# Seven block products instead of eight for the output projections of the long set in a hybrid mLSTM and attention layer

## The chip, the cores and the metric

One core of one Trainium2 chip runs the whole layer. The metric is the device time of one execution, in microseconds (us): 2188.01 us before the change, the median of 3 runs (2187.36 to 2189.47).

## What is computed

The layer is applied to two sets of tokens with the same weights: A, the long set (1024 tokens), and B, the short set (512 tokens). Cut to what matters here:

```python
h = rms_norm(x, pre_w)
cols = einsum('bsd,dc->bsc', h, w_in)                 # d = 1024, some 11,000 columns
y_m = mlstm_mixer(...) * silu(m_z)                    # 1024 wide, two directions
y_a = dilated_attention(...) * silu(a_z)              # 512 wide, three groups of heads
p_m = einsum('bsc,cd->bsd', y_m, w_pm)                # 1024 x 1024
p_a = einsum('bsc,cd->bsd', y_a, w_pa)                #  512 x 1024
g = sigmoid(gate)
merged = g[:, :, 0] * p_m + g[:, :, 1] * p_a
out = einsum('bsd,de->bse', merged, w_out)            # 1024 x 1024
return x + rms_norm(out, post_w)
```

All is float32. The kernel writes each factor of a product as hi + lo, two numbers of TensorE's input type, and computes hi·hi + hi·lo + lo·hi: three matmuls for one (`mm3`, L230). Such a pair is made by ScalarE (ACT: hi is a rounded copy) and VectorE (DVE: lo = x − hi).

## The kernel before, in words

**First stage.** It multiplies A's normed tokens by `w_in`. Here the seven block products of a 2x2 block product (Strassen's scheme in Winograd's form) are already used: a "pair" of column units is one block row of weights, A's two blocks of 512 tokens are the other side, and `unit_pair` (L788) forms seven products of 4 k-tiles each, adding and subtracting their outputs with DVE. The sums of weight blocks that the scheme needs are made on GpSimd (POOL) in `pair_weights` (L768, sums at L782 to L785) and `unit_pair` (L800), from two raw loads `pw_raw`. Eight of these pairs, called "zo", hold A's gates z and o.

**Later stages.** The mLSTM of A, attention of A (`attend`), mLSTM of B (`quad`), attention of B, and `combine`, which mixes B's three attention groups (small operations L2033 to L2043 and mixes L2050, L2056 on DVE, turns on TensorE at L2061). They have many short dependent operations, so TensorE (PE) is kept busy with dense products in between. `Fill` (L137) hands these out in *steps*: one step is one k-tile of a dense product, three matmuls of 128x512. `STEPS` says how many steps go beside each stage, `SHORT` is where the short set's part of `w_in` ends.

The last 512 steps hold the output projections, in this order: A's first 512 tokens, A's second, B. For each block of 512 tokens:
- `proj_m` (in `branches`, L2174): 64 steps, 8 output tiles of 8 k-tiles. The weight unit is 128 x 1024 (512 KB), loaded by POOL's queue into one of two `wraw` buffers and split into a hi and a lo tile (L296 on ACT, L302 on DVE) from a ring of pairs. Each output is evicted by DVE with its gate (L2200).
- `proj_a`: 32 steps, 8 outputs of 4 k-tiles; three DVE operations and an ACT copy for each (L2217 to L2220) make the merged tile's hi and lo.
- `final` (L2239): 64 steps, 8 outputs; for each tile of 128 tokens the two halves are squared on ACT (L2261), multiplied by the norm's weights on DVE as they are evicted (L2263, L2268), the root is taken on POOL (L2267), and two DVE operations add the residual `xo` (L2271).
- `split` (L2129) loads the rows of y and splits them to hi and lo (L2144 on ACT, L2145 on DVE). `along` (L2155) runs such a generator beside the steps of another product: the rows of the next block beside `final`, one every 3 steps.

Dense outputs rotate over two PSUM tiles during attention and over four during B's `combine`. PE's and SP's instructions are issued in the order in which the code is written; those of DVE, ACT and POOL are placed by a scheduler before the run. On each engine the resulting order is fixed: an instruction that waits holds up all behind it.

Of the kernel before, what the change touches and what calls it, by code (L numbers as in the profile page):

```python
# [29 lines left out]
P = 128  # L30
# [174 lines left out]
class Net:  # L205
    def __init__(self, tc, a):
        self.tc, self.nc, self.a = tc, tc.nc, a
        self.clock = self.lag = 0
        self.deep, self.zeros = 1, []
        self.pending, self.owner = [], {}  # L210
        self.defer, self.mixed, self.rows = False, set(), {}
        self.queued, self.pace = [], 1
        self.side = self.nc.sync
        self.lows = None
        self.scans, self.state, self.keyed, self.held, self.sum = [], [], [], [], None
        self.low_part = None
        self.retired = []
        self.narrow, self.acc, self.direct = {}, [None, None], {}
# [568 lines left out]

    def unit_pair(self, weights, H, sb, cp, ps):  # L788
# [189 lines left out]
    def short_units(self, T):  # L978
# [30 lines left out]
        def gate(br, ct):  # L1009
            def use(p):  # L1010
                t = w()
# [1113 lines left out]
    def place(self, which, i, dt=F32R):  # L2125

        return self.take((("V0b", "V1b", "K0", "K1"), ("H0", "H1", "H2", "H3"))[which][i], dt).rearrange("p (k t) -> p k t", k=4)
# [27 lines left out]
    def along(self, units, make, every):  # L2155
# [3 lines left out]
        def wrap(u, last):  # L2159
            def go(weights):  # L2160
                if "g" not in got:
                    got["g"], got["n"] = make(), 0
# [9 lines left out]
        return [wrap(u, u is units[-1]) for u in units]  # L2172

    def branches(self, T, b, odd, before):  # L2174
# [48 lines left out]
        return (self.along(before, lambda: self.split(T, b, 0, [(odd, 0, 1), (odd, 2, 1)], yb, 2 if len(before) > 1 else 3), 3)  # L2223
# [15 lines left out]
    def final(self, T, b):  # L2239
# [4 lines left out]
        def make(weights):  # L2244
            sb = self.osb
            fill = weights.__self__
            self.flush(lambda p: p[3] is not None and p[3][0] is self.sw)
            o = [x[F32] for x in self.sw.bufs]
# [59 lines left out]
STEPS = (316, 260, 192, 290, 86)  # L2308


def body(tc, a):
# [3 lines left out]
    with ExitStack() as st:  # L2315
# [5 lines left out]
        B = Tokens(dram, 512, a[x2], a[y2], "b")  # L2321
        N.constants(N.const)
# [5 lines left out]
        with ExitStack() as s1:  # L2328
# [83 lines left out]
            with ExitStack() as s4:  # L2412
# [16 lines left out]
                with ExitStack() as s3:  # L2429
# [3 lines left out]
                    for kind, i in ([("att", j) for j in range(0, 24, 2)]  # L2433
# [6 lines left out]
                        c = N.unit_pair(weights, H, sb, cp, ps)  # L2440
                        v = [x[:, 1:1 + A.S] for x in c]
# [29 lines left out]
        with ExitStack() as s1:  # L2471
# [35 lines left out]
            with ExitStack() as s2:  # L2507
                sp = N.pool(s1, "sp", 1, "right")
                N.sw = Rot(N, [sp.tile([P, BLK], F32R, name=f"sw{i}") for i in range(4)])
# [29 lines left out]
            extra = [N.take(x) for x in ("X0", "Q1")]  # L2539
            N.wsplit[:0] = [[x[:, 1024 * i:1024 * (i + 1)] for i in range(2)] for x in extra]  # L2540
# [4 lines left out]
            N.postw = None  # L2545
# [21 lines left out]
            N.flush(lambda p: True)  # L2567


def _layout(i):  # L2570
# [13 lines left out]
    def gate_bias(n):  # L2584
# [10 lines left out]
        "w_pm": units(f("w_proj_m")[0], KT), "w_pa": units(f("w_proj_a")[0], 4).reshape(4, 2, P, 4 * P).transpose(0, 2, 1, 3).reshape(4, P, KT * P), "w_out": f("w_out")[0].reshape(4, 2, P, 2, 512).transpose(3, 0, 2, 1, 4).reshape(8, P, KT * P),  # L2595
        "conv": np.concatenate([f("m_conv_w")[0], f("m_conv_b")], 0).reshape(4, 16, P).transpose(2, 1, 0),
# [23 lines left out]
```

## Time and profile before

| | |
|---|---|
| Time, median of 3 (range) | 2188.01 us (2187.36 to 2189.47) |
| Span of the profiled execution | 2185.1 us; the page gives no time of its own for this execution |
| Median less span | 2.9 us |
| TensorE busy | 2173.5 us (99%), 11626 matmuls |
| VectorE / ScalarE / GpSimd busy | 1460.8 (67%) / 1085.1 (50%) / 704.2 us (32%) |
| Weight loads for the outputs | 512 KB each, 24 of `w_pm` and 24 of `w_out` |

The rows name engine, line, operation and tile. "Busy" is time with an instruction in flight; matmuls overlap each other (a 128x512 matmul shows a duration of 389 to 406 ns, while the next starts sooner), so their rate is read from start to start. The same holds, less so, for DVE.

### The profile page before, as it was taken

How to read it: one execution, taken by the hardware profiler on the slowest of the kernel's cores; microseconds unless marked ns; L12 is line 12 of the kernel's file. 1: busy time of each engine (PE TensorE's matmuls, PEld its weight loads, DVE VectorE, ACT ScalarE, POOL GpSimd, SP SyncE). 2: the span in 40 equal slices, each digit the busy share in tenths (PEclk: the TensorE clock that was granted, in tenths of full speed). 3: DMA queues.
4: the chain of work that ended last, by engine and by line, in shares of the span. 5: the costliest groups of instructions: out<-in, count | busy, mean ns of one | idle time of the engine just before them, and what ended most of it. 6: DMA issues, size and time to landing. Idle time of an engine off the chain costs nothing.

```text
span 2185.1 us, 33611 instructions
## 1 busy us (share of the span) xinstructions
PE 2173.5 (99%) x11626; PEld 1857.3 (85%) x11626; DVE 1460.8 (67%) x2927; ACT 1085.1 (50%) x2228; POOL 704.2 (32%) x989
## 2 busy tenths in 40 slices
PE   9999999999999999999999999999999999999998
PEld 8988888888888888888888889999788888888887
DVE  8766564657778555547888775574668855656674
ACT  7322333444444343446777656666756544554332
POOL 1000332333333222326776650011045522232331
PEclk9999999999999999999999999999999999999999
DMA  3642454733333222367646558877668786776772
GB/s 139 193 139 73 146 162 144 227 110 116 107 115 114 75 82 97 135 216 261 202 164 225 175 167 262 240 241 196 203 233 278 248 288 205 229 261 187 242 240 106
DMA packets 205748, 395.62 MB, mean 181 GB/s; under 512 B 36393, under 2 KB 117993, under 8 KB 205578
## 3 DMA queue, kind: packets, MB, share of 16 engines
q1 hardware_dynamic: 175272, 281.39, 40.2%
q0 software_dynamic: 26704, 99.50, 13.8%
q10 hardware_dynamic: 3602, 12.59, 1.4%
q8 instruction: 92, 1.51, 0.3%
q14 instruction: 78, 0.64, 0.1%
HBM read 274.71 MB, written 118.69 MB: 180 GB/s over the span
## 4 chain that ended last, share of the span: by engine, by line
PE 97%; DVE 1%; ACT 1%; DMA 1%; issue 0%; POOL 0%; DVEq 0%; POOLq 0%; ACTq 0%
PE d L233 14%; PE d L235 14%; PE d L234 14%; PE dense L233 13%; PE dense L234 13%; PE dense L235 13%; PE lg L1801 2%; PE pt L1831 2%; PE o L1874 1%; PE num L233 1%; PE num L235 1%; PE num L234 1%; PE num L1494 1%; PE o L1853 1%; PE a L1201 1%; PE kv L233 1%
## 5 line engine op out<-in xcount | busy, mean ns | idle before, releaser
L233 PE MATMUL dense<-H,wh 128*128 128x512 f32 x664 | 269.3, 406 | 0.0
L234 PE MATMUL dense<-H,wh 128*128 128x512 f32 x664 | 260.3, 392 | 0.0
L235 PE MATMUL dense<-H,wl 128*128 128x512 f32 x664 | 260.2, 392 | 0.0
L233 PE MATMUL d<-Hh,phla 128*128 128x512 f32 x608 | 236.5, 389 | 0.0
L235 PE MATMUL d<-Hh,phla 128*128 128x512 f32 x608 | 236.5, 389 | 0.0
L234 PE MATMUL d<-Hl,phla 128*128 128x512 f32 x608 | 236.5, 389 | 0.0
L302 DVE TENSOR_TENSOR wl<-wraw,wh 128x1024 fp32r<-128x1024 f32 (+1 forms) x121 | 150.8, 1248 | 57.9 <-ACT wh L296 57.8
L235 PE MATMUL d<-Hh,phlb 128*128 128x512 f32 x456 | 177.4, 389 | 0.0
L233 PE MATMUL d<-Hh,phlb 128*128 128x512 f32 x456 | 177.4, 389 | 0.0
L234 PE MATMUL d<-Hl,phlb 128*128 128x512 f32 x456 | 177.4, 389 | 0.0
L296 ACT ACTIVATE wh<-wraw 128x1024 fp32r<-128x1024 f32 (+1 forms) x124 | 128.1, 1036 | 62.1 <-PE dense L234 24.3
L235 PEld LDWEIGHTS dense<-H,wl 128*128 128x128 f32 x664 | 124.7, 188 | 28.1
L782 POOL TENSOR_TENSOR psum_w<-pw_raw 128x512 f32<-128x512 f32 x38 | 56.7, 1492 | 271.1 <-DMA pw_raw<-w_in 259.9
L1820 DVE CUSTOM_DVE_ANT_0 ls<-lg,bias 128x256 f32<-128x256 f32 (+2 forms) x240 | 78.7, 350 | 90.3 <-PE lg L1801 61.7
L233 PEld LDWEIGHTS dense<-H,wh 128*128 128x128 f32 x664 | 125.0, 188 | 16.4 <-issue 1.2
L234 PEld LDWEIGHTS dense<-H,wh 128*128 128x128 f32 x664 | 125.2, 189 | 14.7
L235 PEld LDWEIGHTS d<-Hh,phla 128*128 128x128 f32 x608 | 114.1, 188 | 23.7
L234 PEld LDWEIGHTS d<-Hl,phla 128*128 128x128 f32 x608 | 114.1, 188 | 23.7
L233 PEld LDWEIGHTS d<-Hh,phla 128*128 128x128 f32 x608 | 114.1, 188 | 23.7
L800 POOL TENSOR_TENSOR psum_w<-pw_raw,psum_w 128x512 f32<-128x512 f32 x38 | 49.3, 1298 | 254.2 <-DVE phla L764 254.2
L1824 ACT ACTIVATE ls<-ls,nm 128x256 f32<-128x256 f32 (+1 forms) x192 | 87.3, 456 | 70.2 <-DVE nm L1822 47.0
L233 PE MATMUL d<-v,Hh 128*128 128x484 f32 (+1 forms) x336 | 121.3, 361 | 0.1
(665 smaller groups left out, 5838.8 us busy)
## 6 DMA issues: line engine op xcount, KB each, us to landing
pw_raw<-w_in SPq DMA_DIRECT2D x76, 512.0 KB, 3.9
wraw<-w_in SPq DMA_DIRECT2D x63, 512.0 KB, 4.4
aqk_a<-pwk SPq DMA_DIRECT2D x32, 512.0 KB, 6.7
wraw<-w_pm POOLq DMA_DIRECT2D x24, 512.0 KB, 5.9
wraw<-w_out POOLq DMA_DIRECT2D x24, 512.0 KB, 3.7
Q<-aqk_a SPq DMA_DIRECT2D x20, 512.0 KB, 6.3
wraw<-w_v POOLq DMA_DIRECT2D x22, 430.0 KB, 6.5
aqk_b<-sw SPq DMA_DIRECT2D x36, 256.0 KB, 7.2
```

The lines of the kernel that those rows point to most:

```text
L233: nc.tensor.matmul(out, lh, rh, start=start, stop=False, **kw)
L234: nc.tensor.matmul(out, lh, rl, start=False, stop=False, **kw)
L235: nc.tensor.matmul(out, ll, rh, start=False, stop=stop, **kw)
L296: high = nc.scalar.activation(hi[:, :n], raw[:, :n], AF.Copy)
L302: low = (self.lows or nc.vector).tensor_sub(lo[:, :n], raw[:, :n], hi[:, :n].bitcast(F32))
L782: self.nc.gpsimd.tensor_add(s[:, 0], ws[1][:, 0], ws[1][:, 1])
L800: nc.gpsimd.tensor_sub(s[:, 1], wa[:, 1], s[:, 1])
L1201: nc.tensor.matmul(p[:, c - c0], kT[:, ct, c * P:(c + 1) * P], qT[:, ct, c * P:(c + 1) * P], start=ct == 0, stop=ct == 1)
L1801: nc.tensor.matmul(lg[:, hh], q[hh][:, qs], z.rearrange("p (n j) -> p n j", j=P)[:, pair], start=z is k[hh], stop=z is not k[hh])
L1820: nc.vector.tensor_tensor_reduce(out=ls[rows, hh], in0=ts["lg"][hh][rows, of], in1=bt[rows, hh, by], scale=1.0, scalar=NEG, op0=OP.add, op ...
L1824: self.held = self.held[-3:] + [nc.scalar.activation(ls[:, hh], ls[:, hh], AF.Exp, bias=nm[:, hh:hh + 1], accum_out=ot[:, 128 + hh:129 + hh])]
L1831: nc.tensor.transpose(pp[:, hh * nk + x], ts["ls"][:, hh, x * P:(x + 1) * P], self.ident)
```

## The change

`proj_m` and `final` of A are no longer done for each block of 512 tokens. A new function `outputs` does both token blocks at once as a 2x2 block product: for `proj_m`, seven products of 4 outputs and 4 k-tiles (112 steps where there were 128); then `proj_a` for both blocks, with one split of each of its four weight units (64 steps, as before); then `final`, again 112 steps where there were 128. In all there are 1248 steps instead of 1280, and the entry of `STEPS` for B's attention goes from 290 to 258.

- The four sums of weight quadrants for each of the two matrices are made in the first stage by `output_sums`, called in each of the eight "zo" pairs: two loads of 512 KB into `pw_raw` buffers, four POOL operations of 128x512, three stores to a DRAM tile `q_sums`. The raw quadrants come as a new input `w_q`, a rearranged copy of `w_pm` and `w_out`.
- The activations' sums are made on POOL (`combined`, L2248 of the new file, 16 operations of 128x512 for each projection), and every combination is then split by `divide` (ACT L2233, DVE L2234): 28 pieces for each projection, in a ring of 6 places.
- Each product's output is evicted to partial sums: on DVE at L2435 to L2444 in `final`, where one tile can need two additions. Squares, norm and residual follow in `square` (L2414, L2415) and `close` (L2420 to L2424).
- The tiles `mg` (two) hold both the junk output of the squares and one half of the finished tile.
- `place` names other buffers; the four `sw` tiles become one tile and serve as one more pair of the weight ring, where there were two more (X0, Q1).
- B's rows are split beside the new `final`, one every 2 steps from step 86 of its 112.

The diff, cut:

```diff
+    def output_sums(self, i, sb, wk):
...
+        s = wk().rearrange("p (a c) -> p a c", a=2)
+        nc.gpsimd.tensor_add(s[:, 0], wb[:, 0], wb[:, 1])
+        nc.gpsimd.tensor_sub(s[:, 1], s[:, 0], wa[:, 0])
+        nc.gpsimd.tensor_sub(wb[:, 0], wa[:, 0], wb[:, 0])
+        nc.gpsimd.tensor_sub(wa[:, 1], wa[:, 1], s[:, 1])
+        nc.sync.dma_start(self.qs_sums[0:2, u, :, c].rearrange("q p c -> p q c"), s)
...
-    def along(self, units, make, every):
+    def along(self, units, make, every, skip=0):
...
+                    got["g"], got["n"] = make(), -skip
                 for _ in u.make(weights):
-                    if got["n"] % every == 0:
+                    if got["n"] >= 0 and got["n"] % every == 0:
                         next(got["g"], None)
...
+    def outputs(self, T, before):
...
+        def divide(into, key, at, x):
+            hi, lo = at
+            nc.scalar.activation(hi, x, AF.Copy)
+            nc.vector.tensor_sub(lo, x, hi.bitcast(F32))
+            into[key] = at
...
+            jobs += parts(0, a0)
+            two = parts(1, b0)
+            jobs += two[:2] + sums(sub, a1, b1, a1) + two[2:] + sums(add, a0, a0, a1) + parts(2, a0) + sums(sub, b0, b0, a0)
+            jobs += parts(3, a1) + sums(sub, a1, b1, a0)
+            jobs += parts(4, b0) + parts(5, a1) + parts(6, b1)
...
+        def final(weights):
...
+            def square(b, h, t, y, engine):
+                junk = sb.tile([P, S], F32, name="mg", bufs=2)
+                nc.scalar.activation(junk, y, AF.Square, accum_out=ss[b][:, t, h:h + 1])
+                engine.tensor_mul(y, y, pw[:, h * S:(h + 1) * S])
...
+            def evict(i, t, ps):
+                q, r = u[:, t], x[:, t]
+                if i == 0:
+                    nc.scalar.activation(q, ps, AF.Copy)
+                elif i == 1:
+                    self.evicted = add(o[:, t], q, ps)
+                    square(0, 0, t, o[:, t], nc.gpsimd)
+                elif i == 3:
+                    self.evicted = add(r, q, ps)
+                elif i == 4:
+                    y = sb.tile([P, S], F32, name="mg", bufs=2)
+                    self.evicted = add(y, r, ps)
+                    square(0, 1, t, y, nc.vector)
+                    close(0, t, (o[:, t], y))
+                else:
+                    if i == 5:
+                        add(r, r, ps)
+                    self.evicted = add(q, q, ps)
+                    if i == 5:
+                        square(1, 1, t, r, nc.gpsimd)
+                    if i == 6:
+                        square(1, 0, t, q, nc.vector)
+                        close(1, t, (q, r))
...
-        return (self.along(before, lambda: self.split(T, b, 0, [(odd, 0, 1), (odd, 2, 1)], yb, 2 if len(before) > 1 else 3), 3)
+        return (self.along(before, lambda: self.split(T, b, 0, [(odd, 0, 1), (odd, 2, 1)], yb, 3), 2, 86)
...
-STEPS = (316, 260, 192, 290, 86)
+STEPS = (316, 260, 192, 258, 86)
...
+                        if kind == "zo":
+                            N.output_sums(i, sb, w)
...
-            finals = [N.final(*x) for x in ((A, 0), (A, 1), (B, 0))]
-            units = short[:-4] + N.branches(A, 0, 0, short[-4:])
-            units += N.branches(A, 1, 1, finals[:1]) + N.branches(B, 0, 0, finals[1:2]) + finals[2:]
+            last = N.final(B, 0)
+            first, final = N.outputs(A, short[-4:])
+            units = short[:-4] + first + N.branches(B, 0, 0, [final]) + [last]
```

Where the instructions stand. First DVE near the end of A's `final`, beside `combine` of B, in the kernel before. `dense` are the PSUM outputs, `mg` and `sw` the two halves of a finished tile, `xo` the residual, `Q0` and `az1` belong to `combine`:

```order
L2266 SCALAR_TENSOR_TENSOR ss_19916<-ss_19916 128x1
L2268 TENSOR_TENSOR mg_20270<-dense_20197,postw_18670 128x512
L2056 TENSOR_TENSOR Q0_20056<-Q0_20056 128x512
L2271 SCALAR_TENSOR_TENSOR xo00_17492<-sw1_7265,ss_19916,xo00_17492 128x512
L2271 SCALAR_TENSOR_TENSOR xo01_17493<-mg_20215,ss_19916,xo01_17493 128x512
L302 TENSOR_TENSOR wl2_7153<-wraw1_7147,wh2_7152 128x1024
L2063 TENSOR_TENSOR az1_20052<-tp2_20301,az1_20052 128x512
L2056 TENSOR_TENSOR Q0_20056<-Q0_20056 128x512
```

There is one eviction for each output, and a row of B is not split here: that was done beside earlier steps. The same place in the changed kernel, where `dense_20070` is the first and `dense_20177` the last of the fifth product's four outputs, `dense_20302` the last of the sixth's, `dense_20338` the first of the seventh's, and `K0<-ymr0,X0` (L2168) is the lo half of a row of B:

```order
L302 TENSOR_TENSOR wl2_7250<-wraw0_7243,wh2_7249 128x1024
L2168 TENSOR_TENSOR K0_20259<-ymr0_17585,X0_20258 128x512
L2057 TENSOR_TENSOR wd8_20240<-cw8_20235,V0a_20110 128x24
L2444 TENSOR_TENSOR H1_19560<-H1_19560,dense_20338 128x512
L2415 TENSOR_TENSOR mg_20167<-mg_20167,postw_19565 128x512
L2420 SCALAR_TENSOR_TENSOR ss_19563<-ss_19563 128x1
L2438 TENSOR_TENSOR mg_20199<-H0_19562,dense_20177 128x512
L2058 TENSOR_TENSOR wd8_20240<-wd8_20240 128x8
L302 TENSOR_TENSOR wl0_7246<-wraw1_7244,wh0_7245 128x1024
L2443 TENSOR_TENSOR H0_19562<-H0_19562,dense_20302 128x512
L2444 TENSOR_TENSOR H1_19560<-H1_19560,dense_20302 128x512
```

Outputs are now evicted out of turn (`dense_20177` after `dense_20338`), the norms of the fifth product's tiles have moved in among the sixth's and seventh's evictions, and B's rows stand between them. A little later, still on DVE in the changed kernel, stand the last lo halves of B's rows, `H2<-…,H3` (L2168), three ahead of and one behind the norms and mixes:

```order
L302 TENSOR_TENSOR wl1_7248<-wraw1_7244,wh1_7247 128x1024
L2168 TENSOR_TENSOR H2_20261<-sraw_7362,H3_20260 128x512
L2168 TENSOR_TENSOR H2_20261<-ymr0_17585,H3_20260 128x512
L2168 TENSOR_TENSOR H2_20261<-ymr1_17586,H3_20260 128x512
L2424 SCALAR_TENSOR_TENSOR gab_19568<-H1_19560,ss_19564,gab_19568 128x512
...
L2069 TENSOR_TENSOR X1_20112<-V0a_20110,cw8_20496 128x512 x3
L302 TENSOR_TENSOR H0_20477<-wraw1_7244,H0_20477 128x1024
L2168 TENSOR_TENSOR H2_20261<-sraw_7362,H3_20260 128x512
```

These four moved from a place well ahead of A's last evictions to one behind them. On PE, the product that reads them is B's first of `proj_m`, `dense_20487`, right behind A's last output `dense_20434`:

```order
L235 MATMUL dense_20434<-wh1_7247,V1b_19358 128x512
L233 MATMUL dense_20487<-X0_20258,wh2_7249 128x512
L234 MATMUL dense_20487<-K0_20259,wh2_7249 128x512
...
L234 MATMUL dense_20487<-H2_20261,wh2_7249 128x512
L235 MATMUL dense_20487<-H3_20260,wl2_7250 128x512
```

In PE's order 153 matmuls of 128x512 and one turn of four 128x128 lie between the last matmul of `dense_20070`, the fifth product's first output, and the last k-tile of `dense_20487`.

More of the change, by code (lines that the diff above doesn't have):

```diff
@@ L2246, in make @@
             fill = weights.__self__
-            self.flush(lambda p: p[3] is not None and p[3][0] is self.sw)
-            o = [x[F32] for x in self.sw.bufs]
+            o = self.four("V0b")
+            o = [o[:, i] for i in range(4)]
             ss = sb.tile([P, 4, 8], F32, name="ss", bufs=2)
@@ L2321, in body @@
         B = Tokens(dram, 512, a[x2], a[y2], "b")
+        N.qs_sums = dram.tile([4, 4, P, 1024], F32, name="q_sums")
         N.constants(N.const)
@@ L2544, in body @@
             N.xo_bufs = [(i, [N.osb.tile([P, BLK], F32, name=f"xo{i}{j}") for j in range(2)]) for i in range(2)]
-            N.postw = None
+            N.late, N.postw = Rot(N, [x for _, two in N.xo_bufs for x in two]), None
             N.attend(B, fill, STEPS[3], kept["qkv"], ("lg", "o", "pt"), 7)
```

261 lines of the change are left out of this document (254 added, 7 removed).

## The prediction

> **What bounds the kernel now.** I read the page first, then TensorE's waits, then the windows, then single rows.
>
> ```profile
> span 2185.1 us, 33611 instructions
> PE 2173.5 (99%) x11626; PEld 1857.3 (85%) x11626; DVE 1460.8 (67%) x2927; ACT 1085.1 (50%) x2228; POOL 704.2 (32%) x989
> PE   9999999999999999999999999999999999999998
> PE 97%; DVE 1%; ACT 1%; DMA 1%; issue 0%; POOL 0%; DVEq 0%; POOLq 0%; ACTq 0%
> ```
>
> PE is busy in every slice and is 97% of the chain. Its waits say the same:
>
> ```profile
> engine line waited for: us in total, times, longest us
> PE d L2370 <- DMA Hh<-prew: 2.3, 1, 2.3
> PE d L476 <- ACT Hh L470: 0.5, 1, 0.5
> PE d L420 <- DVE u2b L417: 0.5, 1, 0.5
> PE d L235 <- DVE Hl L472: 0.4, 1, 0.4
> ```
>
> All are at the start. So a matmul that goes is time that goes, as long as the others keep up. How close they come is in the windows (after the length: busy us of PE, PEld, DVE, ACT, POOL, then the granted clock):
>
> ```profile
> 450.00:600.00 150.00, 150.00 (x663) 124.20 (x663) 111.61 (x115) 63.63 (x65) 51.53 (x51) 1.00 0.30 106
> 750.00:800.00 50.00, 50.00 (x222) 41.42 (x221) 28.59 (x34) 18.42 (x20) 14.40 (x12) 1.00 0.21 74
> 1050.00:1200.00 150.00, 149.95 (x911) 132.83 (x910) 125.47 (x249) 108.13 (x257) 106.13 (x169) 1.00 0.61 202
> 1850.00:1900.00 50.00, 50.00 (x278) 43.39 (x278) 34.99 (x90) 26.99 (x72) 14.51 (x27) 1.00 0.72 236
> 2060.00:2080.00 20.00, 20.00 (x93) 16.54 (x92) 17.91 (x34) 5.84 (x9) 9.09 (x17) 1.00 0.85 266
> 2160.00:2186.00 26.00, 17.82 (x79) 14.44 (x77) 8.70 (x16) 2.75 (x8) 3.34 (x6) 0.91 0.31 118
> ```
>
> In B's `combine`, from 2060 on, DVE is busy 17.9 of 20 us: the next bound stands there, hidden so far.
>
> **What goes.** 1280 steps become 1248: 32 steps of three matmuls, 96 in all. The first window has 663 matmuls in 150 us, 0.226 us each; near the outputs the starts lie as far apart:
>
> ```profile
> 1900.88 0.39 PE L235 MATMUL dense<-Q,K 128*128 128x512 f32 x1
> 1901.11 0.39 PE L233 MATMUL dense<-Q,K 128*128 128x512 f32 x1
> 1901.33 0.39 PE L234 MATMUL dense<-Q,K 128*128 128x512 f32 x1
> ```
>
> 96 x 0.227 = 21.8 us, all from the path. An output of `final` had 8 steps (24 matmuls, 5.4 us) and has 4 (12 x 0.227 = 2.7 us). The eight weight splits that go (40 for A become 32) lie beside PE and give nothing by themselves.
>
> **What comes, first stage.** Four POOL additions and three stores in each of eight pairs, where POOL has 14.4 of 50 us busy. One addition:
>
> ```profile
> L800 POOL TENSOR_TENSOR psum_w<-pw_raw,psum_w 128x512 f32<-128x512 f32 x38 | 49.3, 1298 | 254.2 <-DVE phla L764 254.2
> ```
>
> A pair is 7 x 4 x 3 = 84 matmuls, 19 us; POOL gets 4 x 1.3 = 5.2 us more in it, about 11 instead of 5.5. The raw loads of the next pair queue behind on the shared buffers, one pair later than now; POOL and SP still have half a pair free. I take 0, and 2 us as the upper end.
>
> **What comes, outputs: DVE's queue.** DVE's prices, start to start, are in B's `combine`:
>
> ```profile
> 2064.58 0.15 DVE L2266 SCALAR_TENSOR_TENSOR ss<-ss 128x1 f32<-128x1 f32 x1
> 2064.65 0.69 DVE L2268 TENSOR_TENSOR mg<-dense,postw 128x512 f32<-128x512 f32 x1
> 2065.25 0.69 DVE L2056 TENSOR_TENSOR Q<-Q 128x512 f32<-128x512 f32 x1
> 2065.85 0.75 DVE L2271 SCALAR_TENSOR_TENSOR xo<-sw,ss,xo 128x512 f32<-128x512 f32 x1
> 2066.51 0.75 DVE L2271 SCALAR_TENSOR_TENSOR xo<-mg,ss,xo 128x512 f32<-128x512 f32 x1
> 2067.18 1.22 DVE L302 TENSOR_TENSOR wl<-wraw,wh 128x1024 fp32r<-128x1024 f32 x1
> 2068.31 0.69 DVE L2063 TENSOR_TENSOR az<-tp,az 128x512 f32<-128x512 f32 x1
> ```
>
> So 0.60 us for 128x512, 0.66 for a residual, 1.13 for the lo half of a weight, and some 0.15 (the first row's duration) for a small operation. Over the whole of A's outputs DVE fits: counted from the code, the new ones need 160 x 0.60 + 16 x 0.66 + 32 x 1.13 + 8 x 0.15 = 144 us for 288 steps (196 us of PE), the old ones 120 us for 320 steps (218 us). B's attention and `combine` come on top. But the load isn't even. Where the norms of both token blocks, B's rows and `combine` meet, I counted DVE's order of the changed kernel from the eviction of `dense_20070` to the last lo half of B's rows: 52 operations of 128x512, 16 residuals, 8 weights, 32 small ones.
>
> 52 x 0.60 + 16 x 0.66 + 8 x 1.13 + 32 x 0.15 = 31.2 + 10.6 + 9.0 + 4.8 = **55.6 us**.
>
> DVE can't begin before `dense_20070` is finished, and PE can't compute the last k-tile of B's first product before the list is done. Between these two PE has 153 matmuls and a turn:
>
> ```profile
> 2065.82 0.44 PE tp L2061 x4
> ```
>
> 153 x 0.227 + 0.44 = **35.2 us**. Hence PE stands still for at least 55.6 − 35.2 = 20.4 us here, whatever it waits for on the way. That nearly equals the saving. More comes on top, since DVE's list isn't free of waits. Two I can work out:
> - At its head: the second output ends 2.7 us after the first, and ahead of its eviction only 0.60 + 0.60 + 0.15 us can be done: 1.4 us idle.
> - The seventh product's pieces go to ring places that the sixth holds: V1b is read by `dense_20302`, the seventh output after `dense_20070`, and its first place is free 6 x 2.73 + 0.7 = 17.1 us on. After the two ACT copies, at 0.60 us each (this square is the nearest row), DVE makes the lo halves until about 19.0 us, where its list alone would be through them at 17.1 us (2.7 us for the second output, 15 x 0.60 + 2 x 0.66 + 2 x 1.13 + 4 x 0.15 = 13.2 us from there, and these two halves, 1.2 us): 1.9 us idle.
>
> ```profile
> 2067.36 0.60 ACT L2261 ACTIVATE mg<-dense 128x512 f32<-128x512 f32 x1 [2.43 <-DVE xo L2271]
> ```
>
> That makes 20.4 + 1.4 + 1.9 = 23.7 us. Then, operations that read what the one before wrote are dearer than 0.60:
>
> ```profile
> 2120.74 0.69 DVE L2217 SCALAR_TENSOR_TENSOR mg<-gab,dense 128x512 f32<-128x512 f32 x1
> 2121.46 0.69 DVE L2218 TENSOR_TENSOR mg<-mg,H 128x512 f32<-128x512 f32 x1
> 2122.07 1.47 DVE L2220 TENSOR_TENSOR V1b<-mg,V0b 128x512 fp32r<-128x512 f32 x2
> ```
>
> 0.72 us from the first to the second, which reads its result, and 0.61 to the next. If a quarter of the 52 are of that kind, it is 13 x 0.12 = 1.6 us; between 0 and 3. And DVE and POOL hold each other up in the first stage (least, median, longest ns):
>
> ```profile
> L785 POOL TENSOR_TENSOR pw_raw<-pw_raw x38: 1287/1292/2277, 224.3 to 909.6; 128x512 f32<-128x512 f32 x38
> L764 DVE TENSOR_TENSOR phla<-pw_raw,phla x38: 1210/1220/2337, 221.3 to 926.3; 128x1024 fp32r<-128x1024 f32 x38
> ```
>
> The same DVE operation takes 1.21 us or up to 2.34: 1.1 us more, which is nearly a POOL addition (1.29). Five or six POOL operations of 128x512 stand in this stretch. At most half of the DVE time is in operations of two SBUF inputs that could meet one: 0 to 6 x 1.1 = 6.6 us, and as the median shows no delay I take 1.5. The Trainium skill, "SBUF — State Buffer", section "SBUF: two separate sides", says that GpSimd and a VectorE operation with two SBUF inputs exclude each other for the whole instruction; the longest durations above agree, the medians don't force it, and by the rule alone the sum would be some 5 us above mine.
>
> Together the stretch costs 23.7 + 1.6 + 1.5 = 26.8 us. Who waits: the first output of the seventh product's second tile, whose PSUM tile is `dense_20177`'s (evicted late because its `mg` buffer must first pass square, root and residual of an earlier tile), some 2.5 us; a turn of `combine`, behind the mixes, about 4 us; the rest at B's first product.
>
> **What comes, the rest of the outputs.** The evictions now come every 2.7 us with up to three operations each. In the sixth product of `proj_m` DVE has 3 x 0.60 + 0.60 for a piece + half a weight for 2.7 us of PE, with attention beside (35 of 50 us busy now, outputs among it): 0 to 3 us. At the twelve changes of product the third and fourth piece's places come free only two steps (1.4 us) ahead of use, about an ACT copy and a lo half: 0 to 6 us. I take 2 us for both. In the window from 1050 PE is unhurt with DVE busy 125 of 150 us, so I stay at the low end.
>
> **Sum.** −21.8 + 26.8 + 2 = +7.0 us. On the span: 2192.1; the median of the runs is 2.9 us above the span, so **2195.0 us**, where 2188.0 stood.
>
> **Rivals.**
> 1. *DVE's list runs faster than its prices* (0.10): with a full queue and no waits DVE starts its operations closer together than in the rows above, and keeps nearer to PE. It decides from a list of 52.6 us on (a stall of 17.4 us, 0.57 us for each 128x512 and the rest as much cheaper). At 0.50 us the list is 46.3 us, the stall 11.1, and with the 2 us elsewhere 8.7 us of the saving stay: **2179**, a gain. For it: PE was unhurt at 125 of 150 us. Against it: the rows from 2064.65 to 2066.51 stand back to back already, at 0.60 us.
> 2. *Just the floor* (0.22): no ring wait, no dearer operations, PE's own waits elsewhere hidden: 20.4 to 22 us, **2187 to 2188**, no change to be measured.
> 3. *TensorE's clock falls in the waits* (0.10). In the last window the granted clock is 0.91 over 26 us in which PE was idle for 8.2; 9% of 26 us is 2.3 us of clock lost. If three waits above 3 us each lose as much, it is 7 us more: **2202**. For it: that row; against it: the clock is 1.00 after the start's waits of up to 2.3 us, in all other windows. The Trainium skill, "TensorE: Matmul & The Clock Gate", section "The HAM clock gate", gives half clock after an idle window of about 3.4 us until as long a busy one; by that, 1.7 us for each wait, 5 us in all.
> 4. *More rows pay* (0.06): ports, product changes and `proj_m` at their upper ends: 23.7 + 3 + 6.6 + 9 + 2 = 44.3, +22.5: **2210**.
>
> **How the numbers follow.** My forecast has 0.52, with 24 to 32 us of stalls: 2190 to 2198. A fifth of it falls below +4.4 us. A measurement of this kernel can tell about 0.2%, 4.4 us, from no change. Faster: rival 1, 0.10. Same: rival 2 and a part of the forecast, 0.22 + 0.08 = 0.30. Slower: the rest, 0.60. The range leaves out rival 1 and a part of rival 4: 2184 to 2210, the lower end below the floor's 2186.6 since 0.58 instead of 0.60 per operation would take 1 us off and small operations may be cheaper.
>
> **What would show it.** PE matmuls of the outputs fewer by 96 at the same 0.227 us. PE's waits, only at the start so far, show a sum of about 29 us, most of it between A's last outputs and B's first product, on DVE `H2` (L2168), `mg`/`H` evictions (L2438, L2444) and a turn; there DVE is 95% busy or more. In the first stage no waits. I am wrong if PE's waits stay under 10 us, if they stand in the first stage, or if DVE has gaps of microseconds while PE waits: then another engine or a load is the bound.

## The result, and the profile after

The changed kernel takes **2214.48 us** (median of 4 runs, 2211.88 to 2215.33) against 2187.72 us: a ratio of 1.0119, 95% interval 1.0105 to 1.0133, or 26.8 us slower. The forecast was 2195.0 us, 7 us slower, with a range up to 2210, which the result exceeds. The sign was right, the size was not.

The page of the changed kernel, the lines that answer to those shown of before:

```profile
span 2212.3 us, 33662 instructions
PE 2165.9 (98%) x11530; PEld 1845.4 (83%) x11530; DVE 1530.8 (69%) x2975; ACT 1092.7 (49%) x2252; POOL 840.2 (38%) x1069
PE   9999999999999999999999999999999999999598
PE 91%; DVE 3%; DMA 2%; issue 2%; ACT 1%; POOL 1%; SPq 0%; DVEq 0%; POOLq 0%; ACTq 0%
```

There are 96 matmuls fewer, as the change says. But PE's time outside matmuls went from 11.6 us (2185.1 − 2173.5) to 46.4 us (2212.3 − 2165.9), 34.8 us more, and the matmuls that are left are busy for only 7.6 us less instead of 21.8: they became 14.2 us dearer. −21.8 + 34.8 + 14.2 = 27.2 us, the difference of the spans. The hole in the slices is the last but two. PE's waits, longest first:

```profile
engine line waited for: us in total, times, longest us
PE dense L233 <- ACT H L2167: 11.5, 1, 11.5
PE dense L234 <- DVE H L2168: 7.4, 2, 7.2
PE dense L233 <- DVE mg L2438: 4.4, 1, 4.4
PE d L2692 <- DMA Hh<-prew: 3.2, 1, 3.2
PE tp L2080 <- DVE wd L2059: 2.0, 1, 2.0
PE lg L1820 <- DVE ot L1839: 1.9, 1, 1.9
PE pt L1850 <- ACT ls L1843: 1.5, 1, 1.5
PE dense L234 <- DVE V0b L2234: 1.5, 1, 1.5
PE dense L235 <- DVE V1b L2234: 1.2, 1, 1.2
```

The first two rows are B's rows at B's first product (11.5 us at its eighth k-tile, 7.2 us at its fifth), the third is the late eviction `mg`, the fifth a turn of `combine`: the four places that the prediction named. The `lg`, `pt`, `V0b` and `V1b` rows are at two others, the start of B's attention and of `proj_m`. In the windows (PE, PEld, DVE, ACT, POOL, granted clock):

```profile
2000.00:2030.00 30.00, 30.00 (x170) 24.22 (x169) 23.47 (x50) 16.28 (x39) 16.27 (x21) 1.00 0.44 146
2030.00:2060.00 30.00, 24.36 (x97) 19.26 (x96) 24.14 (x49) 11.75 (x21) 12.37 (x22) 0.91 0.85 298
2060.00:2080.00 20.00, 12.03 (x44) 9.10 (x43) 19.56 (x33) 9.50 (x22) 12.13 (x14) 0.84 0.50 168
2080.00:2100.00 20.00, 7.09 (x15) 4.80 (x16) 16.26 (x31) 4.03 (x5) 7.54 (x14) 0.59 0.88 325
2100.00:2120.00 20.00, 20.00 (x87) 16.21 (x87) 11.19 (x21) 2.35 (x3) 5.28 (x10) 0.94 0.54 165
```

From 2030 to 2100 PE is idle for 5.6 + 8.0 + 12.9 = 26.5 us, and its clock falls: the 243 matmuls from 2030 to 2120 take 63.5 us of busy time, 0.26 us each. In the chain right behind the last wait one sees it (start, us between starts):

```profile
2097.49 0.79 PE dense L234
2098.28 0.43 PE dense L235
2098.70 0.43 PE dense L233
...
2102.90 0.24 PE dense L233
2103.15 0.23 PE dense L234
```

0.43 us apart for 4.6 us, then 0.23 again. Shorter waits have it too: behind 1.9 us of waiting (to 1785.08) and 1.5 us (to 1787.33) stands the same half rate, until 1791.4, and so it does from 2068.0 to 2071, behind a wait of 2.0 us at the turn:

```profile
1787.33 0.93 PE L1850 MATMUL pt<-ident,ls 128*128 128x128 f32 x4 [1.52 <-ACT ls L1843]
1788.42 0.63 PE L234 MATMUL dense<-H,wh 128*128 128x512 f32 x1
1788.85 0.63 PE L235 MATMUL dense<-H,wl 128*128 128x512 f32 x1
```

DVE's list began at 2030.63 (eviction of `dense_20070`) and its last lo half ended at 2097.43: 66.8 us, where my terms gave 55.6 + 1.4 + 1.9 + 1.6 + 1.5 = 62.0. The window of the list (PE, PEld, DVE, ACT, POOL):

```profile
2030.63:2097.43 66.80, 40.33 (x146) 30.58 (x144) 57.67 (x106) 24.21 (x47) 31.20 (x49) 0.81 0.75 263
```

DVE is busy for 57.7 us and idle for 9.1. On DVE, in order of time, the rows that are longer than their kind, or waited:

```profile
2046.86 0.69 DVE L2168 TENSOR_TENSOR K<-ymr,X 128x512 fp32r<-128x512 f32 x1 [3.22 <-ACT X L2167]
2064.72 1.27 DVE L2415 TENSOR_TENSOR mg<-mg,postw 128x512 f32<-128x512 f32 x1
2069.64 1.22 DVE L2415 TENSOR_TENSOR H<-H,postw 128x512 f32<-128x512 f32 x1
2071.46 3.52 DVE L2415 TENSOR_TENSOR H<-H,postw 128x512 f32<-128x512 f32 x1
2091.82 1.41 DVE L2424 SCALAR_TENSOR_TENSOR xo<-H,ss,xo 128x512 f32<-128x512 f32 x2 [2.81 <-POOL ss L2421]
```

and on POOL at the same times:

```profile
2064.16 1.28 POOL L2415 TENSOR_TENSOR H<-H,postw 128x512 f32<-128x512 f32 x1 [2.25 <-ACT mg L2414]
2069.01 1.29 POOL L2415 TENSOR_TENSOR H<-H,postw 128x512 f32<-128x512 f32 x1
2071.88 2.53 POOL L2415 TENSOR_TENSOR H<-H,postw 128x512 f32<-128x512 f32 x2
```

Each DVE multiplication ends 0.55 to 0.57 us after POOL's ends (2065.99 and 2065.44; 2070.86 and 2070.30; 2074.98 and 2074.41), as if it had begun only then; the third waits so although its row begins 0.42 us ahead of POOL's. 0.6 + 0.5 + 2.8 = 3.9 us are lost so. Of the idle time, 2.8 and 3.2 us are waits for a root and for a row that was loaded late, both in POOL's queue. The last row of B is late too, on POOL and ACT:

```profile
2087.56 0.54 POOL L274 DMA_DIRECT2D sraw<-ym_b  x1
```

```profile
2095.79 0.63 ACT L2167 ACTIVATE H<-sraw 128x512 fp32r<-128x512 f32 x1 [1.42 <-DMA sraw<-ym_b]
```

Its hi half ends at 2096.42; DVE's operation ahead of its lo half ends at 2096.83 (2095.61 + 1.22). So at the end of the wait two things are ready within half a microsecond, DVE's list and a load that POOL's queue issued at 2087.56, and taking away one alone would leave the other.

### The profile page after: what moved, and what is told of

Same layout as the page of the kernel before. It is cut to its first block, busy times and chain, and to the rows that moved or that the text cites. A ratio compares the mean times of both kernels' runs of the same rounds, so it can differ in the third digit from the quotient of the medians.

```text
span 2212.3 us, 33662 instructions
## 1 busy us (share of the span) xinstructions
PE 2165.9 (98%) x11530; PEld 1845.4 (83%) x11530; DVE 1530.8 (69%) x2975; ACT 1092.7 (49%) x2252; POOL 840.2 (38%) x1069
## 4 chain that ended last, share of the span: by engine, by line
PE 91%; DVE 3%; DMA 2%; issue 2%; ACT 1%; POOL 1%; SPq 0%; DVEq 0%; POOLq 0%; ACTq 0%
PE d L233 14%; PE d L235 14%; PE d L234 14%; PE dense L233 12%; PE dense L234 11%; PE dense L235 11%; PE lg L1820 2%; PE pt L1850 1%; PE o L1893 1%; PE num L233 1%; PE num L234 1%; PE num L235 1%; PE num L1513 1%; PE a L1220 1%; PE kv L233 1%
## 5 line engine op out<-in xcount | busy, mean ns | idle before, releaser
L234 PE MATMUL dense<-H,wh 128*128 128x512 f32 x700 | 276.4, 395 | 7.4 <-DVE H L2168 7.4
L233 PE MATMUL dense<-H,wh 128*128 128x512 f32 x660 | 269.3, 408 | 11.5 <-ACT H L2167 11.5
L302 DVE TENSOR_TENSOR wl<-wraw,wh 128x1024 fp32r<-128x1024 f32 (+1 forms) x122 | 156.2, 1282 | 38.1 <-ACT wh L296 38.0
L234 PEld LDWEIGHTS dense<-H,wh 128*128 128x128 f32 x700 | 132.8, 190 | 24.3 <-DVE H L2168 8.3
L782 POOL TENSOR_TENSOR psum_w<-pw_raw 128x512 f32<-128x512 f32 x38 | 61.4, 1617 | 232.9 <-DMA pw_raw<-w_in 215.8
L233 PEld LDWEIGHTS dense<-H,wh 128*128 128x128 f32 x660 | 125.1, 190 | 28.7 <-ACT H L2167 12.2
```

The costliest lines, as they stand in the source:

```text
L233: nc.tensor.matmul(out, lh, rh, start=start, stop=False, **kw)
L234: nc.tensor.matmul(out, lh, rl, start=False, stop=False, **kw)
L302: low = (self.lows or nc.vector).tensor_sub(lo[:, :n], raw[:, :n], hi[:, :n].bitcast(F32))
L782: self.nc.gpsimd.tensor_add(s[:, 0], ws[1][:, 0], ws[1][:, 1])
```

## The experiments

**Theory:** PE stands behind one in-order DVE list. **Rivals:** the clock, PE's own work, loads on POOL's queue, the start of the stage. All times are medians on the same chip as runs of the kernel before (2187.8 to 2188.0 us in all four sets); ratios are to it.

**1. Work in the longest wait** (`repeat_k`):

```diff
...
+                if ct == 0:
+                    for k in 2 * list(range(4)):
+                        c = slice(k * P, (k + 1) * P)
+                        hi, lo = yb[0]
+                        self.mm3(pm, (wm[0][:, c], wm[1][:, c]), (hi[:, k], lo[:, k]), k == 0, k == 3)
```

> The changed kernel with the first four k-tiles of B's first proj_m product computed three times over (24 matmuls more, 5.4 us of TensorE at full clock; the result is the same, the first passes are thrown away). My theory: TensorE stands in a wait of 11.5 us right behind them, so the added work costs nothing: 2212 to 2215 us, and the wait at the fifth k-tile falls by 5 us or more. If the clock that falls in that wait costs time by itself, the busier TensorE saves up to 2 us. Rival (TensorE's own work sets the end there): 2220 us.

2212.95 us (1.0116, 1.0099 to 1.0133): 24 more matmuls cost nothing. PE's own work doesn't set the end there. The expectation named the wrong row of the two: the wait at the fifth k-tile is the one of 7.2 us. It fell to 4.0 us, 3 us less and not 5 or more, since PE also came 1.5 us earlier to the product (2068.87 instead of 2070.41); the wait of 11.5 us, at the eighth, stayed (12.3).

**2. A shorter list** (`no_residual`):

```diff
-                    nc.vector.scalar_tensor_tensor(xt[h], y, s[:, 6:7], xt[h], op0=OP.mult, op1=OP.add)
```

> The changed kernel without the 16 additions of the residual for the long set (its output is then x alone): 16 VectorE operations of 0.66 us, 10.6 us, go from the list; all else stays. My theory (the list of VectorE sets the end of the stretch): 10.6 us less, up to 13.4 us with the wait for the root of 2.8 us that one of them has: 2201 to 2204 us. Rival clock (half clock after the waits makes the loss): 0 to 3 us less. Rival loads (the residual's loads and stores on GpSimd's queue hold B's rows up): the loads stay, so about 3 us less, 2211 us.

2200.09 us (1.0059, 1.0044 to 1.0074): 14.4 us less, a little over the list theory's 10.6 to 13.4, far from the rivals' 0 to 3. The wait isn't gone: PE's longest is now 8.3 us, at a turn.

**3. Other work ahead of the rows** (`front_k`):

```diff
...
-            for ct in range(KT):
...
+            for ct, ks in [(c, range(4)) for c in range(4)] + [(c, range(4, 8)) for c in range(4)] + [(c, range(8)) for c in range(4, 8)]:
...
```

> The changed kernel with B's first four proj_m outputs in two passes: k-tiles 0 to 3 of all four, then k-tiles 4 to 7 of all four (same work, four PSUM tiles). Useful work of 12 steps, 8.2 us, comes ahead of the k-tiles that wait for B's last rows. My theory: the wait there falls from 18.9 us to about 10 and the time by 7 to 10 us: 2205 to 2208 us. If weight splits for four outputs at once lengthen the VectorE list (2 to 3 of 1.13 us moved ahead of the rows) the gain is 4 to 6 us. Rival (the wait only moves to the next product because VectorE stays behind): 2212 to 2215 us.

2204.65 us (1.0079, 1.0064 to 1.0094): 9.8 us less, near the upper end of the theory's 7 to 10. In the two profiled executions PE's waits are 7.3 us shorter and its matmuls 1.5 us cheaper. The list stays, PE just has something to do. (The edit also loads the gates at other places, which the cut doesn't show.)

**4. One part alone** (`proj_m_only`, the diff cut). `final` goes back to the code of before for each block; `proj_a` splits its results as it goes:

```diff
-            last = N.final(B, 0)
-            first, final = N.outputs(A, short[-4:])
+            finals = [N.final(*x) for x in ((A, 0), (A, 1), (B, 0))]
+            first, second = N.outputs(A, short[-4:])
...
-STEPS = (316, 260, 192, 258, 86)
+STEPS = (316, 260, 192, 274, 86)
```

> Only proj_m of the long set as seven products; its final stays two times eight outputs, B's rows are split beside the second of them as before the change. 16 steps fewer than before, 48 matmuls, 10.9 us. My theory (TensorE waits for one in-order VectorE list where the seven-product final, B's rows and combine meet): that list is gone, TensorE has no wait over 2 us near B's first product, and what is left are the waits at the start of proj_m, 3 to 6 us in all: 2180 to 2184 us, faster than before. Rival (the seven-product scheme costs its evictions and pieces wherever it stands, half of the 48 us that came back belong to proj_m): 2195 us or more.

2198.19 us (1.0049, 1.0034 to 1.0064): my theory missed. The waits near B's first product are gone, but 48 matmuls fewer made it 10.2 us *slower*, so 21 us come back at `proj_m` alone. Two causes were in this trace and that of the changed kernel.

**5. SyncE's queue** (`sw_late`). First the changed kernel's queue, then that of before:

```profile
1770.62 5.04 SPq L249 DMA_DIRECT2D gt_b<-sw  x2
1775.75 0.89 SPq L274 DMA_DIRECT2D bias<-erow  x2
```

```profile
1766.10 0.94 SPq L274 DMA_DIRECT2D bias<-erow  x2
```

The change turns `sw` into a weight pair, for which the last gates must be stored first; these stores wait for ACT, and the loads of B's attention are issued behind them, 9.7 us later than before.

```diff
-            N.flush(lambda p: p[3] is not None and p[3][0] is N.sw)
-            sw = N.sw_tile()
+            def swap():
+                N.flush(lambda p: p[3] is not None and p[3][0] is N.sw)
+                sw = N.sw_tile()
...
+            N.hook = 792, swap
```

> The changed kernel, but the sw tile becomes a weight pair only from step 792 on, so that the last two stores of short-set gates out of sw are issued on SyncE's queue behind the first loads of B's attention instead of ahead of them (bias, Q, V1a: issued at 1775.8 us in the changed kernel's trace, 1766.1 us in that of before). Theory: these loads are the cause of TensorE's waits of 1.9 and 1.5 us at 1785 us, of the half clock that follows and of the waits of 1.5 us and less behind it: all go, 4 to 7 us less: 2208 to 2211 us. Rival (fewer dense steps for each call, 258 instead of 290, bare the start of attention; or the weight ring with a pair less for 24 steps costs the same): no difference, 2213 to 2215 us.

2211.9 us (1.0108, 1.0092 to 1.0125): 2.6 us less, short of the 4 to 7 us expected and hardly clear of the scatter, since the interval overlaps that of the changed kernel. The waits on `lg` and `pt` are gone, but that on `V0b` grew from 1.5 to 4.3 us: another cause stood behind.

**6. The same with `proj_m` alone** (`proj_m_sw_late`, with Q1 as a fifth weight pair):

> Only proj_m as seven products, with the sw tile as a weight pair from step 792 on, and Q1 as a fifth pair once its rows are split. The run with proj_m alone took 2198 us, 21 us more than its 48 matmuls fewer would give; its trace has 3.3 us of waits at 1785 us, one of 5.0 us at 1843 us on a piece, 13.7 us at half clock behind them, and 3 us of waits on weight halves after 2000 us. Theory (late loads of attention, and what follows from them in the queues, are most of it): waits of 8 us and half of 13.7 us go, and 2 us on weights: 2181 to 2184 us, faster than before. Rival (the pieces and the double evictions of proj_m are the cause, the start of attention is not): 2194 to 2198 us.

2190.41 us (1.0012, 1.0003 to 1.0022): 7.8 us less than version 4, between the two theories; the two edits weren't separated. (The wait of 5.0 us that the expectation puts at 1843 us ends at 1833.8 in version 4's trace.) One wait of 4.7 us was left, at the first pieces. In its trace DVE and then POOL (L1846 is a small operation of attention that takes 0.16 us in the median of 96, L2253 are the sums):

```profile
1816.73 0.42 DVE L1844 CUSTOM_DVE_ANT_0 ls<-lg,bias 128x256 f32<-128x256 f32 x1
1818.02 5.35 DVE L1846 TENSOR_SCALAR nm<-ot 128x2 f32<-128x2 f32 x1
1823.29 0.68 DVE L2239 TENSOR_TENSOR V1b<-K,V1b 128x512 fp32r<-128x512 f32 x1
```

```profile
1818.37 1.29 POOL L2253 TENSOR_TENSOR K<-K,K 128x512 f32<-128x512 f32 x1
1819.61 1.29 POOL L2253 TENSOR_TENSOR K<-K,H 128x512 f32<-128x512 f32 x1
1820.86 2.48 POOL L2253 TENSOR_TENSOR K<-K,K 128x512 f32<-128x512 f32 x2
```

An operation of 128x2 began 0.35 us ahead of the first of four back-to-back additions and ended at 1823.37, 0.03 us behind the last.

**7. The sums of weights** (`no_sums`):

```diff
...
-                        if kind == "zo":
-                            N.output_sums(i, sb, w)
```

> The changed kernel without the weight sums in the first stage: no loads, additions and stores in the eight zo pairs, and the products read the raw quadrants instead (the outputs of the long set are then not those of the reference). My prediction had 0 to 2 us for them: 2212 to 2215 us. Rival (GpSimd and VectorE hold each other up in the first stage, or the stores crowd its queue): 5 us less or more, 2209 us.

The products read the raw quadrants instead. 2213.26 us (1.0117, 1.0102 to 1.0132): 1.2 us less, inside the 0 to 2 us of the prediction, and no more than the runs scatter.

**8. Multiplications off POOL** (`mul_dve`):

```diff
-                    square(0, 0, t, o[:, t], nc.gpsimd)
+                    square(0, 0, t, o[:, t], nc.vector)
...
-                        square(1, 1, t, r, nc.gpsimd)
+                        square(1, 1, t, r, nc.vector)
```

> The changed kernel with the eight multiplications by the norm's weights that stand on GpSimd moved to VectorE. Four of them lie in the stretch of the long wait, where four VectorE operations took 1.27, 1.22, 1.27 and 3.52 us instead of 0.69. If GpSimd and VectorE exclude each other, VectorE gains 4 us and the 2.8 us in which it waited for a root behind them on GpSimd, and pays 4 x 0.60 us: 3 to 5 us less, 2209 to 2212 us. Rival (they do not exclude each other, the list just gets longer): 2.4 us more, 2217 us.

2202.15 us (1.0066, 1.0051 to 1.0081): **12.3 us less**, with eight operations *more* on DVE. The expectation, 3 to 5 us less, had the sign right and the size far too small. Its multiplications now have their own length, three in 2.25 us:

```profile
2065.40 0.68 DVE L2415 TENSOR_TENSOR mg<-mg,postw 128x512 f32<-128x512 f32 x1
2066.75 2.25 DVE L2415 TENSOR_TENSOR H<-H,postw 128x512 f32<-128x512 f32 x3
```

That is more than the 3.9 us lost to the hold and the 2.8 us on a root. In the two profiled executions, 10.1 us apart, PE's waits are 8.7 us shorter (on ACT `H` 6.3 instead of 11.5 us) and its matmuls 1.4 us cheaper. But more than the hold went: POOL's queue now issues the load of B's last row at 2080.16 instead of 2087.56, and in DVE's order two residuals, three mixes and a weight split that stood ahead of that row's lo half stand behind it. So the 12.3 us aren't the price of the hold alone.

**9. Sums off POOL too** (`sums_dve`):

```diff
-            sub, add = nc.gpsimd.tensor_sub, nc.gpsimd.tensor_add
+            sub, add = nc.vector.tensor_sub, nc.vector.tensor_add
```

> The changed kernel with the eight multiplications and the 32 sums of activations on VectorE instead of GpSimd. To be compared with the run that moved the multiplications alone (2202.2 us). Theory port (while GpSimd runs its additions back to back, a VectorE operation waits them out: one of 0.16 us took 5.35 us at 1818 us in the run with proj_m alone): VectorE gets 32 x 0.60 = 19 us more work, but the waits on pieces at the start of proj_m (V0b, V1b, 2.7 us, and the half clock behind) go: 2196 to 2200 us. Theory queue (VectorE's time is simply too short, wherever the work comes from): 19 us more on a queue that is 75 to 85% busy beside A's outputs, 2205 us or more.

2195.98 us (1.0041, 1.0026 to 1.0056): another 6.2 us less, with 32 operations, some 19 us, more on DVE. Its busy time nevertheless fell, from 1536.6 to 1532.1 us: the other operations became shorter in sum, by more than the new ones take.

**10. The same with `proj_m` alone** (`proj_m_sums_dve`):

> Only proj_m as seven products, sw later, Q1 as a fifth pair (2190.4 us so far), and now its 16 sums on VectorE instead of GpSimd. Theory port: the wait of 4.7 us at 1826 us, in which VectorE's small operation stood 5.35 us behind four back-to-back GpSimd additions, goes, and the 6.8 us at half clock with it: 6 to 8 us less, 2182 to 2185 us, faster than before. Theory queue: 9.6 us more for VectorE, the wait stays or grows: 2190 to 2194 us.

**2183.52 us (0.9983, 0.9974 to 0.9993), faster than before by 4.4 us**, the only version that is. PE's waits are back at the start, but for a turn and four of 0.6 us and less:

```profile
PE d L2633 <- DMA Hh<-prew: 3.3, 1, 3.3
PE tp L2085 <- DVE wd L2064: 1.8, 1, 1.8
PE dense L238 <- DVE H L2325: 0.7, 2, 0.4
PE dense L238 <- DVE H L2525: 0.6, 1, 0.6
PE dense L238 <- DVE mg L2530: 0.5, 1, 0.5
```

**11. Additions that nobody needs** (`dummy_add`, on version 10). Were the sums on POOL merely late?

```diff
+                    nc.gpsimd.tensor_add(s, out[:, k], out[:, k])
```

> The fastest version so far (proj_m alone as seven products, its sums on VectorE, 2183.5 us) with 16 additions of 128x512 on GpSimd beside the sums, whose result nobody reads (each adds the sum's result to itself into an unused buffer). Theory port (an addition on GpSimd holds VectorE up): the wait at the pieces comes back, 4 to 7 us more, 2187 to 2191 us. Rival (the sums on GpSimd were only late, 1.30 us instead of 0.60 each, and the pieces behind them with them): nobody waits for these, 2183 to 2185 us.

2193.85 us (1.0029, 1.0019 to 1.0038): 10.3 us *more*, above the theory's 4 to 7. That the sums were merely late is out as the only cause. Two lo halves, 0.69 us each where nothing holds them, took 4.5 us beside POOL's additions:

```profile
1821.95 4.47 DVE L2239 TENSOR_TENSOR V0b<-K,V0b 128x512 fp32r<-128x512 f32 x2
```

**12. As long a queue without reads** (`dummy_set`, 40 memsets of 20.2 us in all in the trace, against 19.4 us for the 16 additions):

```diff
+                    for z in range(2 + k % 2):
+                        nc.gpsimd.memset(s, 0.0)
```

> The same with 40 memsets of 128x512 on GpSimd (about 0.5 us each, 20 us in all, as the 16 additions), which read nothing from SBUF. Theory port (only a GpSimd operation that reads SBUF holds VectorE up): 2183 to 2186 us. Rival (GpSimd's queue is the cause: weights, gates and rows are issued late behind anything that stands there): as much as with the additions, 2187 us or more.

2186.32 us (0.9993, 0.9984 to 1.0002): 2.8 us more than version 10, between theory and rival, with intervals that overlap. Most of the cost is that of operations that read; a smaller part may be POOL's queue, and with it the gain is no longer clear of noise.

**13. B's rows earlier** (`rows_early`, on version 8):

```diff
...
-yb, 3), 2, 86)
+yb, 3), 2, 66)
```

The second four rows' buffers are also taken only when they are free.

> The changed kernel with the multiplications on VectorE, and B's rows split from step 66 and 82 of A's final instead of 86 and 100 (the second four's buffers are taken only when they are free). To be compared with 2202.2 us. Theory: TensorE's wait at B's first product (6.3 and 2.6 us) hangs on the place of these eight splits behind A's norms in VectorE's queue and on the late loads of the rows on GpSimd's; with them earlier it falls below 3 us in all, 5 to 9 us less: 2193 to 2197 us. Rival (the list is as long as before, the wait moves to the evictions and turns ahead of it): 2200 to 2203 us.

2202.34 us (1.0071, 1.0056 to 1.0086): no change, the rival's forecast. PE no longer waits for rows, but 12.2 and 4.9 us at turns.

**14. Everything** (`all_five`, versions 3, 5, 8, 9, 13 together):

> All changes together on the changed kernel: multiplications and sums on VectorE, rows split earlier, sw as a weight pair later, B's first four outputs in two passes. If the costs add: 2202.2 less 4 (sums), 7 (rows), 2.6 (sw), 2 (what the two passes can still hide) = 2186 to 2188 us, the time of before. If they overlap (each hides the same wait at B's first product): 2191 to 2196 us. Faster than 2183 us only if the half clock goes altogether.

2188.19 us (1.0000, 0.9991 to 1.0009): the time of before. The total of the expectation's sum came out, its parts didn't: the sums brought 6.2 us where it had 4, and the rows nothing by themselves where it had 7. So the agreement is luck. One wait carries most of what is left:

```profile
PE tp L2085 <- DVE wd L2065: 14.3, 1, 14.3
```

**15. That turn later** (`turns_274`, and `turns_split`: 98 steps in 22 shares):

```diff
-STEPS = (316, 260, 192, 258, 86)
+STEPS = (316, 260, 192, 274, 80)
```

> All five changes (2188.2 us), with 274 steps beside B's attention and 80 beside combine: combine's first turn stands 16 steps later in TensorE's order. In the run with all five TensorE waited 14.3 us at that turn, whose mix stands behind A's norms in VectorE's queue, with 17 us at half clock. Theory (only this one turn is early; behind it stands 20 us of work that waits for nothing): 10.9 us of steps come ahead of it, the wait falls below 5 us, and the time by 8 to 14 us: 2174 to 2180 us. Rival (VectorE's list sets the end, the wait moves to the next turn or eviction): 2185 to 2190 us.

> All five changes, with combine's first two turns given four shares of steps instead of two (98 steps in 22 shares instead of 86 in 18): the first turn stands about 9 steps later, the last one 12 steps later, attention as in all five. Theory: 6 to 9 us less than 2188.2, 2179 to 2182 us. Rival: no change, 2185 to 2190 us.

2190.09 us (1.0009, 1.0000 to 1.0019) and 2190.87 us (1.0013, 1.0004 to 1.0022): no gain, as the rivals had it. In `turns_274` the wait moves:

```profile
PE dense L238 <- DVE mg L2449: 8.5, 2, 7.9
PE tp L2085 <- DVE X L2080: 7.2, 1, 7.2
```

Together 15.7 us where there were 14.3 at the turn and 1.9 at `mg`. In `turns_split` it stays at a turn, 16.1 us. The list is too long, wherever in it PE waits.

## Why the prediction failed, step by step

- **What goes, 21.8 us:** right, 96 matmuls; but that every one left costs 0.227 us was not: they became 14.2 us dearer in all. Some 46 of them start 0.43 us apart behind the waits, which makes 46 x 0.20 = 9.2 us, an estimate from these starts; the rest isn't resolved. Rival 3, the clock, priced at 7 us and 0.10, came true *with* the forecast instead of apart from it. Its point against, clock 1.00 after waits of up to 2.3 us at the start, doesn't carry over: here the half rate stands behind a pair of waits of 1.9 and 1.5 us too (at 1788), and behind one of 2.0 us (at 2068). The half clock of the Trainium skill's clock gate ("TensorE: Matmul & The Clock Gate", "The HAM clock gate") agrees with 0.43 against 0.23 us, and 4.6 us of it follow the last wait, where the page has some 3.4.
- **First stage, 0 us:** right within what the runs tell (version 7).
- **The floor, 20.4 us:** right in kind. Version 1 shows that PE's work doesn't set the end, 2 and 3 that the list does (with the last row's load half a microsecond ahead of its end); 13, where the rows come early and nothing is gained, and 15 show that the list does so wherever the wait is put. Rivals 1 and 2 are out. The operations of the list took 57.7 − 3.9 = 53.8 us without the hold, where the terms had 55.6 + 1.6. The 0.15 us for a small operation was too much: in the prediction's own rows the next one starts 0.07 us behind it (2064.58 to 2064.65), 2.6 us less for 32.
- **The failing steps** are the matmuls at 0.227 us throughout, just named, and the waits in DVE's list, in which POOL has a part. The changed kernel is 27.2 us slower by the spans where the sum had 7.0. Of the 20.2 us between, 14.2 are the dearer matmuls, which the sum put at nothing, and 6.0 are PE's waits, 34.8 us where it had 26.8 + 2. In the list, "DVE and POOL hold each other up … I take 1.5" came to 3.9 us: I read medians from the first stage and priced it for one stretch only. The idle time in the list, 1.4 + 1.9 us in the prediction, came to 9.1 us; the root's and the row's waits of 2.8 and 3.2 us on POOL's queue had no term. With that, a sign of being wrong that the prediction names came true: DVE stood still for 2.8 us, until 2091.82, while PE waited. DVE was 86% busy in the list, not 95% or more.
- **What POOL's part costs in all.** Taking POOL's eight multiplications away brought 12.3 us (with another order of loads and of DVE's list), and its sums, half of them at `proj_m` far from the stretch, another 6.2. The rule that I set beside the hold (the Trainium skill, "SBUF — State Buffer", "SBUF: two separate sides": GpSimd and a VectorE operation with two SBUF inputs exclude each other for the whole instruction) agrees with the rows at 2064 to 2075, where each DVE multiplication ends behind POOL's. The hold of 5.35 us goes beyond it: it lasted for four additions, not for one instruction. Why is open. The longest durations in the rows quoted were the better price than the medians.
- **The rest of the outputs, 2 us:** too small. 6.1 us of waits (`lg`, `pt`, `V0b`, `V1b`) stand there. A first cause, the stores of `sw` ahead of attention's loads on SyncE's queue, was in the order of the changed kernel, and I didn't cost it. The waits on `lg` and `pt` go with it (version 5), but the 2.6 us of that version are hardly clear of noise; the 7.8 us of version 6 are with `proj_m` alone and a fifth weight pair.
- **The chances:** a fifth of the forecast's 0.52 is 0.10, where the working has 0.08; nothing hangs on it. The result lies above rival 4's 2210 too, whose upper ends had no term for the clock or for POOL's queue.

Taken one after the other, the versions bring 12.3 us (POOL's multiplications, version 8), 6.2 us (its sums, 9) and 7.8 us (rows, `sw` and two passes together, 14), 26.3 of the 26.8 us. That isn't a sum of separate prices: the 7.8 us are what the last step brought as a whole, where its parts alone brought 0, 2.6 and 9.8 us on other versions. What stays open is how the 12.3 us divide between hold, POOL's queue, the order of DVE's list and clock. That B's rows by their place and late loads cost nothing of their own is shown only with the multiplications on DVE (version 13).

## What to carry to other kernels

Moving elementwise work to an idle GpSimd isn't free when VectorE is nearly full: look for VectorE rows that are longer than their kind and end just after a GpSimd row, and price the move by them. Where two engines meet in one place, sum each engine's in-order list between two fixed points, not its share of the whole; a wait that is moved along such a list comes back elsewhere. And in a kernel bound by TensorE a stall can cost more than its length: behind four stalls of 2.0 to 11.5 us here, and behind a pair of 1.9 and 1.5 us, matmuls ran at half rate for some 3 to 5 us. Saved matmuls pay only if the stalls stay short.

## What the runs showed of the hardware

- A VectorE operation of 128x2 took 5.35 us instead of 0.16 beside four GpSimd additions in a row (version 6): the hold can reach small operations, and here lasted for the whole run of additions, not for one.
- GpSimd memsets of the same total length (20.2 us, against 19.4 us of additions) cost 2.8 us where the additions cost 10.3 (versions 11 and 12).
- Behind waits of 4 us and more TensorE's matmuls of 128x512 start 0.43 us apart for about 5 us (2055.72 to 2061.00, 2097.49 to 2102.12), then 0.23. Behind two waits of 1.9 and 1.5 us, 0.7 us of matmuls apart, they did so until 1791.41. But not every such wait has it: in version 10 none follows the 1.8 us at a turn.
